# Norms by columns beside the last two output blocks of a stage, every second block of h by GpSimd and ScalarE

## The chip, the cores and the metric

The kernel runs on one core of a Trainium2 chip. The metric is the device time of one execution in microseconds (us); the times of several executions are given as median and span. "PE" is TensorE, "DVE" is VectorE, "ACT" is ScalarE, "POOL" is GpSimd, "SP" is the engine that issues most DMAs.

## The reference, cut to what matters

A backbone of two layers on 256 context tokens and 512 latent tokens, with a model width D of 1024. Cut to what the change touches:

```python
def rmsnorm(x, w):
    xf = x.astype(jnp.float32)
    y = xf * lax.rsqrt(jnp.mean(xf * xf, axis=-1, keepdims=True) + NORM_EPS)
    return (y * w.astype(jnp.float32)).astype(x.dtype)

for l in range(DEPTH):
    hx = modulate(rmsnorm(x, norm1_w[l]), mod_x[0], mod_x[1])      # h * (1 + scale) + shift
    hc = modulate(rmsnorm(ctx, norm1_w[l]), mod_c[0], mod_c[1])
    mix_x, mix_c = token_mixing(hx, hc, w_in[l], ...)
    x = x + mod_x[2] * (mix_x @ w_out[l])
    x = x + mod_x[5] * channel_mlp(modulate(rmsnorm(x, norm2_w[l]), mod_x[3], mod_x[4]), mlp_w1[l], mlp_w2[l])
    if not last:
        ctx = ctx + mod_c[2] * (mix_c @ w_out[l])
        ctx = ctx + mod_c[5] * channel_mlp(modulate(rmsnorm(ctx, norm2_w[l]), mod_c[3], mod_c[4]), mlp_w1[l], mlp_w2[l])
return rmsnorm(x, final_norm_w)
```

The context has a modulation of its own (`mod_c`). The last layer carries the latent tokens alone past its mixing. Everything is fp32; `channel_mlp` is a squared ReLU between two products.

## The kernel before

Tokens lie in columns: columns 0 to 255 are the context, 256 to 767 the latent tokens. The residual stream is eight tiles `X[k]` of 128 rows (features) and 768 columns (`NT`). Weights come in blocks of 128 output features.

**Products.** An fp32 product is made from fp32r parts. A weight block is split by ACT (`whi`, a rounded copy) and DVE (`wlo`, the rest) in halves of four 128-row blocks (`wsplit`, lines 463 to 475; `wload`, 478 to 489, also issues the block's DMA). The activations are split the same way into `hhi` and `hlo`. Each block k then takes three matmuls, hi times hi, lo times hi, hi times lo. A column segment is at most 512 wide, so 768 columns are two segments, 256 and 512 wide (`ALL`); in the last layer after its mixing there is one, of 512 (`LAT`). `gemm` (L492) runs over halves of the weights, segments, k and the three parts. `gemm_pair` (L506) makes two output blocks at once and has k as its outer loop, so that it can start on h of block 0 while block 1 is being made.

**Norms.** While the blocks n of a product are added to the residual stream (`residual`, L273), `sumsq` (L227) squares them on ACT and adds the squares on DVE; after block 7 two matmuls per segment with a matrix of ones (`nrm`) sum over the rows and spread the sum over all rows. `modulated` (L244) then makes `rstd` from it by a Ln and an Exp on ACT, and for each of eight blocks and each segment: `hy` (DVE, x times scale times rstd), `hhi` (ACT, hy plus shift, rounded), `hlo` (DVE, the rest). `hy` has two buffers (pool `tp`, tag `ta`), which the blocks take in turn. DVE makes two of the three steps.

**The four places.** A norm ends and an h begins at (a) the start of layer 0 (near 44 us of the span), where x is read from memory and the sums come from another path; (b) the second norm of layer 0 (606 us), between `w_out` and the MLP; (c) the first norm of layer 1 (1160 us), between the MLP and the input projection, whose first `gemm_pair` makes 32 gate columns and 128 columns of k; (d) the second norm of layer 1 (1590 us), with one segment. At (c) the tiles of layer 0's MLP give way to pools of layer 1.

**Other work there.** In layer 0 a generator `ada_sums` (L359) makes the modulation of layer 1 from 96 blocks of `ada_w` read by DMA: DVE instructions `adacc` over 128x1024, one or two to a block, are put between other work, a step at each `next(sums, None)`. At (a) ACT also issues the eight DMAs that save x to memory (`xd`, L625).

**Order.** Each engine runs its instructions in order. That order is set at build time by a list scheduler that takes the program's dependencies and pools; waits between engines are on semaphores that count finished instructions. So an instruction that waits holds up all that stands behind it on its engine.

Of the kernel before, what the change touches and what calls it, by code (L numbers as in the profile page):

```python
# [140 lines left out]
def flow_kernel(ctx, tc, t, out, dbg=None, stop=None):  # L141
# [85 lines left out]
    def sumsq(k, acc, segs, pl):  # L227

        cols = slice(segs[0][0], NT)
        sq = pl.tile([128, NT], F32, tag="sqa" if k == 0 else "tc", name="sq", bufs=1 if k == 0 else 2)  # L230
        act_(sq[:, cols], X[k][:, cols], AF.Square)
        if k in (0, 7):
            acc.append(sq)
        else:
# [4 lines left out]
        for i, sq in enumerate(acc):
            for c0, cn in segs:  # L240
                if i == 0:
                    o[bank(c0)] = ps("nrm")
                mm(o[bank(c0)][:, 0:cn], ones, sq[:, c0:c0 + cn], i == 0, i == 1)
        return o  # L244

    def modulated(l, which, segs, o, tp):
# [4 lines left out]
        V.tensor_scalar(out=sc, in0=mod[l][:, base + 8:base + 16, :], scalar1=1.0, scalar2=None, op0=ADD)
        tt(sc, sc, bc(prm[l][:, r0:r0 + 8], 2, 2), MUL)
        res = []
        r = tp.tile([128, GAP + 4], F32, tag="tb", name="rstd", bufs=2 - which)
        for c0, cn in segs:
            rr = r[:, c0:c0 + cn]
            act_(rr, o[bank(c0)][:, 0:cn], AF.Ln, scale=1.0 / D, bias=eps)
            act_(rr, rr, AF.Exp, scale=-0.5)
        for k in range(8):
            hi = hpool.tile([128, NT], F32R, tag="hi", name="hhi")  # L260
            lo = hpool.tile([128, NT], F32R, tag="lo", name="hlo")
            y = tp.tile([128, GAP + 4], F32, tag="ta", name="hy")
            for c0, cn in segs:
# [242 lines left out]
    def gemm_pair(w2, acts, segs, n):  # L506

        outs = [{bank(c0): ps("mm") for c0, cn in segs} for _ in n]
        for k in range(8):
            ahi, alo = acts[k]  # L510
            for i, w_ in enumerate(w2):
                whi, wlo = w_[k // 4]
                for c0, cn in segs:
                    for pi, (w, a) in enumerate(((whi, ahi), (whi, alo), (wlo, ahi))):
                        mm(outs[i][bank(c0)][0:n[i], 0:cn], w[:, k % 4, 0:n[i]], a[:, c0:c0 + cn],
                           start=(k == 0 and pi == 0), stop=(k == 7 and pi == 2))
        return outs

# [78 lines left out]
    for l in range(DEPTH):  # L597
# [23 lines left out]
        h = modulated(l, 0, ALL, nrm, tp)  # L621
        del nrm
# [9 lines left out]
        o, o_k0 = gemm_pair(ahead, h, ALL, (32, 128))  # L632
# [904 lines left out]
        acc = []  # L1537
# [1 line left out]
        for n in range(8):
# [2 lines left out]
            nrm = sumsq(n, acc, osegs, tp)
# [6 lines left out]
        h2 = modulated(l, 1, osegs, nrm, tp)  # L1549
        first = gemm_pair(w2, h2, osegs, (128, 128))  # L1550
        acc = []
        for fb in range(4):
            hid = []
            for f in range(8):
                if fb == 0 and f < 2:
                    o = first[f]
# [67 lines left out]
```

## Time and profile before

| what | value |
|---|---|
| median of 3 runs | 1973.41 us (1973.05 to 1975.29) |
| the profiled execution | 1960.3 us |
| its span (first to last instruction in the profile) | 1958.5 us |
| PE busy | 1881.4 us, 96% of the span |
| DVE busy | 1196.3 us, 61% |
| ACT busy | 754.2 us, 39% |
| POOL busy | 101.1 us, 5% |

The span is the part of an execution that the profile's rows cover. A busy share of PE says only that a matmul was under way; matmuls overlap, and a matmul at a lower clock counts as busy for longer. So what PE loses at one place is read from the distance between starts of its matmuls there.

### The profile page before, as it was taken

Reading aid. Unit: us, or ns where it says so; the run is one execution under the profiler, and the core shown is the slowest. Engines: PE = TensorE matmul, PEld = TensorE weight load, DVE = VectorE, ACT = ScalarE, POOL = GpSimd, SP = SyncE. Lnnn points to the kernel's source line nnn. Section 1 sums busy time; section 2 is a strip of 40 time slices with the busy share of each in tenths; the row PEclk is TensorE's granted clock in tenths of the full one; section 3 lists DMA queues with packets and bytes.
Section 4 is the critical chain, followed back from the end, with each engine's and each line's share of the span. In section 5 each row is a group of like instructions: output and inputs, shape, how many; then the busy total and the mean of one; then the engine's idle time right before and its main releaser. Section 6 shows DMA issues by size and latency. Waiting matters only on the chain.

```text
span 1958.5 us, 33935 instructions
## 1 busy us (share of the span) xinstructions
PE 1881.4 (96%) x14107; PEld 1539.8 (79%) x14107; DVE 1196.3 (61%) x2210; ACT 754.2 (39%) x1528; POOL 101.1 (5%) x163
## 2 busy tenths in 40 slices
PE   6999999999899999999999999999999999999998
PEld 3877778778777888888888878677777778888887
DVE  3878875666659566435535349788777754444443
ACT  4652234455424312312213236534355543333242
POOL 0021210000000000000000000212100000000001
PEclk8999989999799999999999999999999999999999
DMA  9220001111364345335423222201011323333332
GB/s 324 80 52 24 23 13 44 57 55 44 120 203 128 109 140 147 94 116 151 129 84 122 81 62 54 63 23 34 23 44 33 102 76 103 97 97 97 97 97 76
DMA packets 225634, 172.28 MB, mean 88 GB/s; under 512 B 19042, under 2 KB 207816, under 8 KB 225480
## 3 DMA queue, kind: packets, MB, share of 16 engines
q1 hardware_dynamic: 219104, 153.38, 26.5%
q10 hardware_dynamic: 4680, 10.70, 1.5%
q0 software_dynamic: 1696, 6.03, 0.9%
q8 instruction: 110, 1.80, 0.4%
q14 instruction: 44, 0.36, 0.1%
HBM read 162.75 MB, written 7.34 MB: 87 GB/s over the span
## 4 chain that ended last, share of the span: by engine, by line
PE 82%; DVE 10%; ACT 4%; DMA 3%; issue 1%; POOL 0%; DVEq 0%; ACTq 0%; SPq 0%; POOLq 0%
PE mm L179 63%; PE mmt L179 2%; PE num L179 1%; PE ops L179 1%; DVE kq L188 1%; DMA wst<-w_in 1%; PE pv L179 1%; DVE wlo L185 1%; PE yt L179 1%; DVE Y L185 1%; PE adaps L179 1%; PE pT L1340 1%; PE t L179 1%; PE Eps L179 1%; PE yps L179 1%
## 5 line engine op out<-in xcount | busy, mean ns | idle before, releaser
L182 ACT ACTIVATE whi<-wst 128x512 fp32r<-128x512 f32 (+1 forms) x388 | 241.7, 627 | 682.2 <-PE mm L179 623.5
L179 PE MATMUL mm<-hhi,whi 128*128 128x512 f32 (+3 forms) x1344 | 477.8, 361 | 12.8 <-ACT hhi L182 11.4
L179 PE MATMUL mm<-hlo,whi 128*128 128x512 f32 (+3 forms) x1344 | 479.4, 357 | 1.5 <-DVE hlo L188 1.3
L179 PE MATMUL mm<-hhi,wlo 128*128 128x512 f32 (+3 forms) x1344 | 475.3, 356 | 0.1
L185 DVE TENSOR_TENSOR wlo<-wst,whi 128x512 fp32r<-128x512 f32 (+1 forms) x388 | 265.1, 687 | 313.3 <-ACT whi L182 309.4
L179 PEld LDWEIGHTS mm<-hhi,whi 128*128 128x128 f32 (+1 forms) x1344 | 251.9, 188 | 55.4 <-ACT hhi L182 14.9
L179 PEld LDWEIGHTS mm<-hlo,whi 128*128 128x128 f32 (+1 forms) x1344 | 253.1, 188 | 39.9 <-DVE hlo L188 3.6
L179 PEld LDWEIGHTS mm<-hhi,wlo 128*128 128x128 f32 (+1 forms) x1344 | 252.2, 188 | 39.0 <-issue 2.8
L179 PE MATMUL mm<-fhi,whi 128*128 128x512 f32 (+1 forms) x784 | 276.0, 352 | 0.0
L179 PE MATMUL mm<-flo,whi 128*128 128x512 f32 (+1 forms) x784 | 276.0, 352 | 0.0
L179 PE MATMUL mm<-fhi,wlo 128*128 128x512 f32 (+1 forms) x784 | 274.6, 350 | 0.0
L188 DVE SCALAR_TENSOR_TENSOR x<-mm,mod,x 128x256 f32<-128x256 f32 (+1 forms) x122 | 79.7, 653 | 142.4 <-PE mm L179 142.3
L179 PEld LDWEIGHTS mm<-fhi,whi 128*128 128x128 f32 x784 | 148.4, 189 | 21.7 <-ACT whi L182 0.8
L179 PEld LDWEIGHTS mm<-fhi,wlo 128*128 128x128 f32 x784 | 148.1, 189 | 19.7
L179 PEld LDWEIGHTS mm<-flo,whi 128*128 128x128 f32 x784 | 148.4, 189 | 19.2
L188 DVE SCALAR_TENSOR_TENSOR adacc<-adw,scT,adacc 128x1024 f32<-128x1024 f32 x84 | 105.8, 1281 | 28.3 <-DMA adw<-ada_w 28.2
L185 DVE TENSOR_TENSOR flo<-r,fhi 128x768 fp32r<-128x768 f32 (+1 forms) x64 | 52.6, 824 | 39.2 <-ACT fhi L182 39.1
L182 ACT ACTIVATE fhi<-r 128x768 fp32r<-128x768 f32 (+1 forms) x64 | 47.2, 740 | 66.8 <-DVE r L185 66.8
L179 PE MATMUL mm<-mlo,whi 128*128 128x512 f32 (+1 forms) x192 | 71.0, 370 | 1.3 <-DVE mlo L185 1.3
L179 PE MATMUL mm<-mhi,whi 128*128 128x512 f32 (+1 forms) x192 | 70.6, 368 | 0.4 <-ACT mhi L182 0.4
L179 PE MATMUL mm<-mhi,wlo 128*128 128x512 f32 (+1 forms) x192 | 70.0, 365 | 0.0
L182 ACT ACTIVATE r<-mm 128x256 f32<-128x256 f32 (+1 forms) x96 | 49.1, 514 | 31.5 <-PE mm L179 31.5
(404 smaller groups left out, 2712.3 us busy)
## 6 DMA issues: line engine op xcount, KB each, us to landing
wst<-mlp_w SPq DMA_DIRECT2D x128, 512.0 KB, 4.0
adw<-ada_w SPq DMA_DIRECT2D x96, 512.0 KB, 4.3
wst<-w_in SPq DMA_DIRECT2D x44, 512.0 KB, 3.7
wst<-w_out SPq DMA_DIRECT2D x64, 128.0 KB, 3.1
xd<-x ACTq DMA_DIRECT2D x8, 384.0 KB, 3.5
x<-xd POOLq DMA_DIRECT2D x8, 384.0 KB, 5.2
xs<-x ACTq DMA_DIRECT2D x4, 512.0 KB, 6.9
wst<-w_in SPq DMA_DIRECT2D x8, 256.0 KB, 3.4
```

What stands on the lines that cost most here:

```text
L179: T.matmul(o, lhsT=l, rhs=r, start=start, stop=stop)
L182: S.activation(out=o, in_=i, func=f, **kw)
L185: (eng or V).tensor_tensor(out=o, in0=a, in1=b, op=op)
L188: V.scalar_tensor_tensor(out=o, in0=a, scalar=s, in1=b, op0=op0, op1=op1)
L1340: T.transpose(o[:, 256 * i + 128 * g:256 * i + 128 * g + 128], Ps[g][:, 128 * (i0 + i):128 * (i0 + i) + 128], ident)
```

## The change

- `sumsq` works per column segment and keeps one sum for each; the matmuls with ones move to `norm_sum`, called per segment. `modulated` is now called per segment, too.
- `last_pair` (new) makes the last two output blocks (6 and 7) of `w_out` in both layers, and of the second MLP product of layer 0, by columns: the first segment of both blocks, then the second segment of both. The norm of the first segment is issued with the second segment's products, its h behind them.
- Segments are now 512 latent columns, then 256 of the context (`LATF`), and at (d) two times 256 (`HALVES`). `gemm_pair` runs per segment, once for each, and h of the second segment is made beside the first segment's products.
- Every second block of h (odd k) is made in another way: GpSimd multiplies x by rstd, ACT scales and shifts it in place, ACT copies it rounded (`hhi`), DVE subtracts (`hlo`). Even blocks stay as they were. Of an odd block DVE now has one instruction, ACT two, GpSimd one.
- The steps of `ada_sums` left over are drained ahead of the last pair of layer 0's MLP; in the loop over `w_out` the eight steps are spread over six blocks rather than eight.

```diff
+LATF = ((256, 512), (0, 256))
-    def modulated(l, which, segs, o, tp):
+    def modulation(l, which):
...
-        r = tp.tile([128, GAP + 4], F32, tag="tb", name="rstd", bufs=2 - which)
...
-            y = tp.tile([128, GAP + 4], F32, tag="ta", name="hy")
-            for c0, cn in segs:
-                m = 1 if c0 == 0 else 0
-                s_ = slice(c0, c0 + cn)
...
+        def modulated(seg, o, pl, bufs):
...
+            act_(r, o[:, 0:cn], AF.Ln, scale=1.0 / D, bias=eps)
+            act_(r, r, AF.Exp, scale=-0.5)
+            for k in range(8):
...
+                y = pl.tile([128, GAP + 4], F32, tag="ta", name="hy", bufs=2)[:, 0:cn]
                 sh = mod[l][:, base + k, m:m + 1]
-                stt(y[:, s_], X[k][:, s_], sc[:, k, m:m + 1], r[:, s_], MUL, MUL)
-                act_(hi[:, s_], y[:, s_], AF.Identity, bias=sh)
-                stt(lo[:, s_], y[:, s_], sh, hi[:, s_].bitcast(F32), ADD, SUB)
+                if k % 2:
+                    tt(y, X[k][:, s_], r, MUL, eng=G)
+                    act_(y, y, AF.Identity, scale=sc[:, k, m:m + 1], bias=sh)
+                    act_(hi[:, s_], y, AF.Copy)
+                    tt(lo[:, s_], y, hi[:, s_].bitcast(F32), SUB)
+                else:
+                    stt(y, X[k][:, s_], sc[:, k, m:m + 1], r, MUL, MUL)
+                    act_(hi[:, s_], y, AF.Identity, bias=sh)
+                    stt(lo[:, s_], y, sh, hi[:, s_].bitcast(F32), ADD, SUB)
...
+    def last_pair(w2, acts, l, g, segs, acc, pl, mk):
...
+        for i, seg in enumerate(segs):
+            for n in (6, 7):
+                o = gemm(None, acts, (seg,), w2=w2[n - 6])
+                if i and n == 6:
+                    o_n = norm_sum(acc, segs[0])
+                if i and n == 7:
+                    h_ = mk(segs[0], o_n, pl, 1)
+                residual(o, l, n, g, (seg,))
+                sumsq(n, acc, ((i, seg),), pl)
+        return h_
...
-        h = modulated(l, 0, ALL, nrm, tp)
-        del nrm
+        if l == 0:
+            mk = modulation(0, 0)
+            h = mk(LATF[0], nrm[1], tp, 2)
+        first = gemm_pair(ahead, h, LATF[0], (32, 128))
+        mk(LATF[1], nrm[0], tp, 2)
+        first = [{1: a, 0: b} for a, b in zip(first, gemm_pair(ahead, h, LATF[1], (32, 128)))]
...
+        steps = HALVES if last else LATF
-        for n in range(8):
+        for n in range(6):
...
-            for _ in range((2, 1, 1, 1, 1, 1, 1, 0)[n]):
+            for _ in range((2, 1, 1, 1, 1, 2)[n]):
                 next(sums, None)
...
+        mk = modulation(l, 1)
+        h2 = last_pair([wload([t["w_out"][l][:, 128 * n:128 * n + 128]], MIXK) for n in (6, 7)], mh, l, 16, steps, acc, tp, mk)
...
-        first = gemm_pair(w2, h2, osegs, (128, 128))
+        first = [gemm_pair(w2, h2, steps[0], (128, 128))]
+        mk(steps[1], norm_sum(acc, steps[1]), tp, 1)
+        first.append(gemm_pair(w2, h2, steps[1], (128, 128)))
...
+            w2 = [wload([t["mlp_w2"][l][3072:4096, 128 * n:128 * n + 128]]) for n in (6, 7)]
+            if not last:
+                for _ in sums:
+                    pass
+                mk = modulation(l + 1, 0)
+                h = last_pair(w2, hid, l, 40, LATF, acc, tp, mk)
+                nrm = {0: norm_sum(acc, LATF[1])}
```

VectorE at (b), before (names are tile and buffer number; `hy` and `hlo` of two blocks in turn, L188 is the helper for scalar-tensor-tensor, x2 two such instructions in a row, `adacc` the sums of `ada_sums`):

```order
L188 SCALAR_TENSOR_TENSOR x_6486<-mm_7077,mod0_121,x_6486 128x512
L185 TENSOR_TENSOR wlo_7368<-wst_7361,whi_7367 128x512
L188 SCALAR_TENSOR_TENSOR adacc_7344<-adw_7501,scT_89,adacc_7344 128x1024 x2
L188 SCALAR_TENSOR_TENSOR hy_7166<-x_6479,sc_7156,rstd_7159 128x256
L188 SCALAR_TENSOR_TENSOR hy_7175<-x_6480,sc_7156,rstd_7159 128x256
L188 SCALAR_TENSOR_TENSOR hy_7166<-x_6479,sc_7156,rstd_7159 128x512
L188 SCALAR_TENSOR_TENSOR hlo_7165<-hy_7166,mod0_121,hhi_7164 128x256
L188 SCALAR_TENSOR_TENSOR hlo_7174<-hy_7175,mod0_121,hhi_7173 128x256
L188 SCALAR_TENSOR_TENSOR hy_7175<-x_6480,sc_7156,rstd_7159 128x512
L188 SCALAR_TENSOR_TENSOR hlo_7165<-hy_7166,mod0_121,hhi_7164 128x512
L188 SCALAR_TENSOR_TENSOR adacc_7344<-adw_7573,scT_89,adacc_7344 128x1024
```

and with the change, from the same place on (L189 is now that helper, L186 the one for tensor-tensor):

```order
L186 TENSOR_TENSOR wlo_7420<-wst_7417,whi_7419 128x512
L189 SCALAR_TENSOR_TENSOR x_6503<-mm_7147,mod0_121,x_6503 128x256
L189 SCALAR_TENSOR_TENSOR adacc_7400<-adw_7557,scT_89,adacc_7400 128x1024
L189 SCALAR_TENSOR_TENSOR hlo_7176<-hy_7177,mod0_121,hhi_7175 128x512
L186 TENSOR_TENSOR hlo_7182<-hy_7183,hhi_7181 128x512
L189 SCALAR_TENSOR_TENSOR hy_7190<-x_6498,sc_7029,rstd_7172 128x512
L186 TENSOR_TENSOR wlo_7424<-wst_7417,whi_7423 128x512
L189 SCALAR_TENSOR_TENSOR adacc_7400<-adw_7629,scT_89,adacc_7400 128x1024
L189 SCALAR_TENSOR_TENSOR hlo_7189<-hy_7190,mod0_121,hhi_7188 128x512
L186 TENSOR_TENSOR hlo_7195<-hy_7196,hhi_7194 128x512
L189 SCALAR_TENSOR_TENSOR hy_7203<-x_6500,sc_7029,rstd_7172 128x512
L189 SCALAR_TENSOR_TENSOR adacc_7400<-adw_7629,scT_89,adacc_7400 128x1024
```

Before, one `adacc` stands between the instructions of the first h blocks; now three or four stand among those of the first four blocks, and the `hlo` of an odd block (a L186 row that reads `hy` and `hhi` alone) stands behind one or two of them.

ScalarE at (b) with the change (L183 is the helper for activations; an `hy` made from `hy` is the in-place scaling of an odd block, an `hhi` with one name its rounded copy):

```order
L183 ACTIVATE rstd_7172<-nrm_7140,cst_85 128x512
L183 ACTIVATE rstd_7172<-rstd_7172 128x512
L183 ACTIVATE whi_7419<-wst_7417 128x512
L183 ACTIVATE hy_7183<-hy_7183,mod0_121,sc_7029 128x512
L183 ACTIVATE hhi_7175<-hy_7177,mod0_121 128x512
L183 ACTIVATE hhi_7181<-hy_7183 128x512
L183 ACTIVATE sq_7228<-x_6503 128x256
L183 ACTIVATE whi_7423<-wst_7417 128x512
L183 ACTIVATE hy_7196<-hy_7196,mod0_121,sc_7029 128x512
L183 ACTIVATE hhi_7188<-hy_7190,mod0_121 128x512
```

Before, ACT had one `hhi` per block and segment there; now three instructions stand for two blocks, in the order odd scaling, even `hhi`, odd `hhi`.

TensorE at (c) with the change (`mm_11876` is the gate product, 32 columns of weights, `mm_11877` the k product of the same segment, 128 columns; `mm_11965` and `mm_11966` are those of the second segment):

```order
L180 MATMUL mm_11876<-hhi_11815,wlo_11863 32x512
L180 MATMUL mm_11876<-hhi_11822,whi_11862 32x512
L180 MATMUL mm_11876<-hlo_11823,whi_11862 32x512
L180 MATMUL mm_11876<-hhi_11822,wlo_11863 32x512
L180 MATMUL mm_11876<-hhi_11828,whi_11862 32x512
L180 MATMUL mm_11876<-hlo_11829,whi_11862 32x512
L180 MATMUL mm_11876<-hhi_11828,wlo_11863 32x512
L180 MATMUL mm_11877<-hhi_11783,whi_11868 128x512
L180 MATMUL mm_11877<-hlo_11784,whi_11868 128x512
L180 MATMUL mm_11965<-hhi_11783,whi_11858 32x256
L180 MATMUL mm_11965<-hlo_11784,whi_11858 32x256
```

Before, the two products of a block followed each other for each k; now the gate product runs over all eight blocks of the first segment ahead of the first matmul of the k product.

## Rows read from the trace of the kernel before

**Rows 1.** The page: the span, and busy time, share and instructions of each engine.
```profile
span 1958.5 us, 33935 instructions
PE 1881.4 (96%) x14107; PEld 1539.8 (79%) x14107; DVE 1196.3 (61%) x2210; ACT 754.2 (39%) x1528; POOL 101.1 (5%) x163
```

**Rows 2.** Windows: length, then busy us (instructions) of PE, PEld, DVE, ACT, POOL, PE clock, DMA, GB/s.
```profile
44.00:52.00 8.00, 7.40 (x26) 5.11 (x27) 8.00 (x16) 3.90 (x8) 0.20 (x2) 0.56 0.95 315
612.00:622.00 10.00, 9.17 (x48) 7.26 (x48) 10.00 (x19) 5.29 (x10) 0.00 (x0) 1.00 0.13 47
```

**Rows 3.** PE timeline, the norm's first matmuls at (b), (c), (d): start, us, instruction.
```profile
606.20 1.03 PE L179 MATMUL nrm<-sq,ones 128*128 128x256 f32 x3
...
1160.39 1.03 PE L179 MATMUL nrm<-sq,ones 128*128 128x256 f32 x3
...
1590.39 1.02 PE L179 MATMUL nrm<-sq,ones 128*128 128x512 f32 x2
```

**Rows 4.** PE timeline, first product of h at (a) to (d), [idle before, releaser].
```profile
44.41 0.42 PE L179 MATMUL mm<-hhi,whi 128*32 128x256 f32 x1 [4.21 <-ACT hhi L182]
...
611.67 0.38 PE L179 MATMUL mm<-hhi,whi 128*128 128x256 f32 x1 [1.84 <-ACT hhi L182]
...
1166.10 0.31 PE L179 MATMUL mm<-hhi,whi 128*32 128x256 f32 x1 [2.21 <-ACT hhi L182]
...
1596.22 0.96 PE L179 MATMUL mm<-hhi,whi 128*128 128x512 f32 x3 [2.98 <-ACT hhi L182]
```

**Rows 5.** PE timeline, the last matmuls of gemm_pair or of the third product.
```profile
64.21 0.40 PE L179 MATMUL mm<-hhi,wlo 128*128 128x512 f32 x1
...
638.72 0.39 PE L179 MATMUL mm<-hhi,wlo 128*128 128x512 f32 x1
638.95 0.28 PE L179 MATMUL mm<-hhi,whi 128*128 128x256 f32 x1
639.06 0.28 PE L179 MATMUL mm<-hlo,whi 128*128 128x256 f32 x1
...
1185.13 0.40 PE L179 MATMUL mm<-hhi,wlo 128*128 128x512 f32 x1
...
1614.14 0.39 PE L179 MATMUL mm<-hhi,wlo 128*128 128x512 f32 x1
```

**Rows 6.** ACT timeline around the four places.
```profile
48.98 0.81 ACTq L625 DMA_DIRECT2D xd<-x  x2
...
1165.56 0.50 ACT L182 ACTIVATE hhi<-hy,mod 128x256 fp32r<-128x256 f32 x1
...
1593.28 0.69 ACT L182 ACTIVATE rstd<-nrm,cst 128x512 f32<-128x512 f32 x1 [1.22 <-PE nrm L179]
1594.00 0.63 ACT L182 ACTIVATE rstd<-rstd 128x512 f32<-128x512 f32 x1
...
1598.31 1.38 ACT L182 ACTIVATE hhi<-hy,mod 128x512 fp32r<-128x512 f32 x2 [1.48 <-DVE hy L188]
...
1604.39 0.61 ACT L182 ACTIVATE whi<-wst 128x512 fp32r<-128x512 f32 x1
```

**Rows 7.** DVE timeline at (b) and (d).
```profile
611.92 0.87 DVE L188 SCALAR_TENSOR_TENSOR hlo<-hy,mod,hhi 128x256 fp32r<-128x256 f32 x2
...
614.03 1.28 DVE L188 SCALAR_TENSOR_TENSOR adacc<-adw,scT,adacc 128x1024 f32<-128x1024 f32 x1
...
1599.07 1.41 DVE L188 SCALAR_TENSOR_TENSOR hlo<-hy,mod,hhi 128x512 fp32r<-128x512 f32 x2
```

**Rows 8.** POOL groups by line and form: count, busy us, mean ns, idle before.
```profile
L185 POOL TENSOR_TENSOR N<-E,cst 128x512 f32<-128x512 f32 x12 | 15.5, 1293 | 46.2 <-ACT E L182 46.1
```

**Rows 9.** Timeline, POOL and DVE in the mixing of layer 0; DVE alone at (d).
```profile
164.15 2.73 POOL L185 TENSOR_TENSOR Nl<-N,Nh 64x512 f16<-64x512 f32 x2 [16.95 <-PE nw L179]
164.61 1.25 DVE L185 TENSOR_TENSOR wlo<-wst,whi 128x512 fp32r<-128x512 f32 x1
...
1603.90 0.69 DVE L185 TENSOR_TENSOR wlo<-wst,whi 128x512 fp32r<-128x512 f32 x1 [1.21 <-PE mm L179]
```

More of the change, by code (lines that the diff above doesn't have):

```diff
@@ L504, in gemm, with gemm_pair @@
         return outs
-    def gemm_pair(w2, acts, segs, n):
-        outs = [{bank(c0): ps("mm") for c0, cn in segs} for _ in n]
+    def gemm_pair(w2, acts, seg, n):
+        outs = [ps("mm") for _ in n]
+        c0, cn = seg
         for k in range(8):
             ahi, alo = acts[k]
-            for i, w_ in enumerate(w2):
+            for o, n_, w_ in zip(outs, n, w2):
                 whi, wlo = w_[k // 4]
[L513 to L516, printed above, removed]
-        return outs
+                for pi, (w, a) in enumerate(((whi, ahi), (whi, alo), (wlo, ahi))):
+                    mm(o[0:n_, 0:cn], w[:, k % 4, 0:n_], a[:, c0:c0 + cn],
+                       start=(k == 0 and pi == 0), stop=(k == 7 and pi == 2))
+        return outs
+    def last_pair(w2, acts, l, g, segs, acc, pl, mk):
[9 more added lines that the diff above has]
+        return h_
     def gemm_tok(l, c0, pairs, hk, evac):
@@ L631, in flow_kernel @@
         zg = temp("ta")
-        o, o_k0 = gemm_pair(ahead, h, ALL, (32, 128))
+        o, o_k0 = first
         evac(zg[0:32], o, ALL, 32)
@@ L1536, in flow_kernel @@
             nc.gpsimd.dma_start(out=X[k][:, ow], in_=xd[k, :, ow])
[L1537 removed]
+        acc = {}
         sums = ada_sums(todo, adp)
[L1539 removed]
+        steps = HALVES if last else LATF
+        for n in range(6):
             o = gemm([t["w_out"][l][:, 128 * n:128 * n + 128]], mh, osegs, order=MIXK, w2=w_next.pop() if w_next else None)
             residual(o, l, n, 16, osegs)
[L1542 to L1543 removed]
+            sumsq(n, acc, tuple(enumerate(steps)), tp)
+            for _ in range((2, 1, 1, 1, 1, 2)[n]):
                 next(sums, None)
@@ L1555, in flow_kernel @@
                 if fb == 0 and f < 2:
-                    o = first[f]
+                    o = [(x[f], seg) for x, seg in zip(first, steps)]
                 else:
                     o = gemm([t["mlp_w1"][l][:, 1024 * fb + 128 * f:1024 * fb + 128 * f + 128]], h2, osegs)
+                    o = [(o[bank(c0)], (c0, cn)) for c0, cn in osegs]
                 r = tp.tile([128, NT], F32, tag="tc", name="r")
-                for c0, cn in osegs:
-                    act_(r[:, c0:c0 + cn], o[bank(c0)][:, 0:cn], AF.Relu)
+                for x, (c0, cn) in o:
+                    act_(r[:, c0:c0 + cn], x[:, 0:cn], AF.Relu)
                 tt(r[:, ow], r[:, ow], r[:, ow], MUL)
@@ L1568, in flow_kernel @@
                 next(sums, None)
-            tail = last and fb == 3
-            for n in range(6 if tail else 8):
+            for n in range(6 if fb == 3 else 8):
                 o = gemm([t["mlp_w2"][l][1024 * fb:1024 * fb + 1024, 128 * n:128 * n + 128]], hid, osegs)
                 residual(o, l, n, 40, osegs)
-                if tail:
+                if fb == 3 and last:
                     finish(n, acc, tp, *LAT[0])
                 elif fb == 3:
-                    nrm = sumsq(n, acc, osegs, tp)
+                    sumsq(n, acc, tuple(enumerate(LATF)), tp)
                 next(sums, None)
-            if tail:
-                w2 = [wload([t["mlp_w2"][l][3072:4096, 128 * n:128 * n + 128]]) for n in (6, 7)]
+            if fb < 3:
+                continue
+            w2 = [wload([t["mlp_w2"][l][3072:4096, 128 * n:128 * n + 128]]) for n in (6, 7)]
[5 more added lines that the diff above has]
+                nrm = {0: norm_sum(acc, LATF[1])}
+            else:
                 for seg in HALVES:
```

54 lines of the change are left out of this document (28 added, 26 removed).

## The prediction

> **What bounds the kernel now.** I read the page first: PE is busy 96% of a span of 1958.5 us, DVE 61%, POOL 5% [rows 1]. So only time in which PE waits, or steps slower than it can, is to be had. The page cannot say where that is; the PE timeline can. Full steps between matmul starts are 0.23 us for 512 columns and 0.115 us for 256 [rows 5]. The change touches four places, and I compare each with what its matmuls need at those steps: 8.3 us for 24 matmuls of both widths (one output block over 768 columns).
>
> At (a) gemm_pair's 48 matmuls of each width need 16.6 us and take from 44.41 to 64.44: 3.4 us more, behind a first wait of 4.2 [rows 4, 5]; the granted clock is 0.56 there and DVE is busy for 8.00 us of 8 [rows 2]. At (b) the norm starts at 606.20 and the third product ends at 638.95: 32.75 us for 2.6 of norm matmuls (about 0.22 and 0.43 for each half of one, two halves a matmul [rows 3]) and 24.9 of products, 5.2 lost. At (c), 1160.39 to 1185.36, 25.0 us for 2.6 and 16.6: 5.8 lost. At (d), 1590.39 to 1614.37, 24.0 us for 1.7 and 16.4: 5.9 lost. The first product's wait ends on ACT's `hhi` in all four, 1.84 to 4.21 us [rows 4]; after it h comes slowly. At (b) DVE is busy all of the 10 us after the norm [rows 2]: DVE makes h there. In all, some 24 us are lost, 1.2% of the span: the most that the change can gain, and less by (a)'s first wait, which it does not touch.
>
> **The column split.** It takes matmuls of 5.7 us (24 of 256 columns for each of n = 6 and 7) out from before the norm and puts them beside it. Call T0 the moment when the first segment of n = 7 is through: 5.7 us before the norm's start of today, so 600.5 at (b), 1154.7 at (c), 1584.7 at (d) [rows 3]. From T0 the kernel before takes 38.4, 30.7 and 29.7 us to the ends named above. The norm of the first segment waits for n = 6's second half on PE, 2.8 us, then takes 1.7 itself (0.9 for 256 columns), then Ln 0.69 and Exp 0.63 on ACT [rows 6] (0.9 together for 256 columns): `rstd` at T0+6.1, at (d) T0+4.9. Only 2.8 us of products are then left to cover h. The split's other additions cost little: the same columns are multiplied, but at (d) as 256 wide (0.115 for half of 0.23), under 0.5 us in all.
>
> **How fast h comes now.** An odd block is a chain through three engines, and `hy` still has two buffers, of which the odd blocks always get the second. So GpSimd cannot start block 3 before DVE has finished block 1's `hlo`. Nothing of two odd blocks overlaps, and the chain is the period for two blocks. For 512 columns: GpSimd's product 1.29, the nearest row being its `N` of the same shape [rows 8]; ACT's scaling and the even `hhi` that stands behind it, 1.38 as two `hhi` take [rows 6]; the rounded copy, 0.54 more, as a `whi` of 0.61 less its overlap [rows 6]; `hlo` 0.69, as `wlo` [rows 9]; three handovers of 0.05. That is 4.05.
>
> To this I add a collision. When DVE's `wlo` ran beside GpSimd's `Nl`, it took 1.25 instead of 0.69 [rows 9]: two-input work of the two engines does not run side by side. An even `hy` on DVE (0.66 a step, half of a pair of 1.41 [rows 7]) is released by the same event as GpSimd's product. I let one wait for the other: 4.7 us a pair. The row bounds it: nothing, to the whole 0.66. I take the whole, since `wlo` was held for nearly its own length. [...]
>
> For 256 columns the same chain is 0.40 + 0.63 (half of 1.29) + 0.50 + 0.40 + 0.30 + 0.40 + 0.15 = 2.8 [rows 6, 7, 8]. PE needs 12 matmuls for two blocks, 2.7 us at 512 and 1.4 at 256. So h is the limit throughout, by 2.0 and 1.4 us a pair. Before, DVE made h at 2.8 us for two blocks of 512 columns, four steps of 0.7 [rows 7].
>
> **Place by place.**
> (a) No split here, the first wait stays. On ACT five `xd` issues stand between the first `hhi` and the first odd scaling, 0.4 us each, 2.0 in all [rows 6]. With `hy` from 43.0, as now, block 1 is whole at 49.0 (0.66 + 1.29 + 2.0 + 0.72 + 0.61 + 0.69). ACT's even `hhi` is not in the chain here, so three pairs of 4.0 and four of 2.5 follow, and 0.5 of matmuls: 71.5 against 64.4, **+7.1**.
> (b) The scheduler put up to two `adacc` of 1.2 us [rows 7] into each pair on DVE. The first pair takes 4.7, two of them (2.4) and a `whi` (0.5): T0+13.7. Three more pairs with 0.8 us each that the chain does not hide, 5.5: T0+30.2. Four pairs of the second segment at 3.0: T0+42.2. Behind the last `hlo` stand 1.4 of the pair and 4.1 of the third product: T0+47.7 against 38.4, **+9.3**.
> (c) Block 1 at T0+10.8, three pairs of 4.7: T0+24.9. The second block of weights waits for the last `hlo` of this segment, since its pool lies where the old stage's `hy` was; so up to then PE has only the 32-wide gate products (24 steps of 0.23, 5.5 us). Then `whi`, 0.8 with handovers, 24 steps of 512 and 48 of 256 columns, 11.2, and 1.8 for steps at half clock after so idle a stretch (as (d) now: 18.15 us from its first product for 16.4 [rows 4, 5]): T0+38.7 against 30.7, **+8.0**.
> (d) Block 1 at T0+7.9, three pairs and four of 2.9: T0+28.2, and 4.1 behind: T0+32.3 against 29.7, **+2.6**.
>
> The sum is 7.1 + 9.3 + 8.0 + 2.6 = **+27.0**. The profiled execution took 1960.3, 13.1 below the median of the runs, 1973.4; it would go to 1987.3. I put the difference on the median: 1973.4 + 27.0, **2000 us**. Differences within 0.2%, 3.9 us, count as none.
>
> **Rivals.**
> *No collision.* GpSimd's product starts at once and costs 1.29: 0.66 less for each of twelve pairs of 512 columns and 0.4 for each of sixteen of 256, 14.3 less: 1986. For it: the collision rows are of other shapes and another stage. Against: both engines wait for the same release here.
> *The cover works, a faster kernel.* GpSimd and ACT take half of h from DVE, and a pair comes in under the 2.7 us that PE needs; then only the first pair is late, by 4.7 less 2.7. (b), (c) and (d) lose 2.0 us each in place of 5.2, 5.8 and 5.9, (a) stays: 10.9 less, 1963. It decides at a period of 2.7 us; the chain is 4.05 before any collision, and only a third `hy` buffer or shorter instructions could bring it there. For it: DVE was the limit at (b) and has two instructions fewer for two blocks.
> *Between the two.* With the even `hhi` out of the chain's way a period would be about 3.4, half way between 4.05 and 2.7, and so half way between 1986 and 1963: about 1975, no change.
> *The clock stays low.* [...] If it falls in all four places while h comes in steps, the dense matmuls behind the last `hlo`, 5.5 + 9 + 4 us, run partly at twice the step: some 8 us more, 2008.
>
> **Chances.** Forecast 0.45, no collision 0.25, clock low 0.10, cover works 0.11, between 0.09. Slower is the sum of the first three, 0.80; within 0.2% 0.09; faster 0.11. The range leaves out the faster case and half of what is between, and reaches at the top past the low clock: 1974 to 2014.
>
> **What would show it.** Right: in the changed kernel's PE timeline pairs of blocks come 4 to 5.5 us apart at 512 columns, with waits on `hhi` or `hlo` of odd blocks; POOL's `hy` starts right after an odd `hlo`; at (c) the first 128-wide product stands 24 us behind T0. Wrong: pairs at 2.7 us, PE without gaps, POOL's products overlapping the odd block before. If GpSimd's product takes much less than 1.29, or DVE's instructions keep their length beside it, the sizes fall first.

## The result and the profile after

The changed kernel takes 2000.94 us, median of 4 runs (1992.20 to 2005.93); the kernel before, beside it, 1973.23 (1972.71 to 1975.29). The ratio is 1.0134, 95% interval 1.0097 to 1.0170: slower by 1.3%. The forecast was 2000. The profiled execution took 1992.2 us, its span is 31.9 us longer than that of [rows 1].

The page of the changed kernel, span and engines (PE, PEld, DVE, ACT, POOL):

```profile
span 1990.4 us, 34272 instructions
...
PE 1889.3 (95%) x14207; PEld 1543.8 (78%) x14207; DVE 1204.2 (61%) x2214; ACT 774.8 (39%) x1596; POOL 140.3 (7%) x195
```

The work went to POOL and ACT as intended: POOL has 39 us more, ACT 21. DVE is not relieved: 8 us more, although 32 products of h are POOL's now. What DVE kept takes longer; how much is counted below, at `odd_on_dve`.

Where the time went is read from PE's first matmul of each stage. Stages in us, each from the start of one such matmul to that of the next; "fc" is the forecast for the place.

| stage | before | after | difference | fc |
|---|---|---|---|---|
| (a) to the gates' transposes, layer 0 | 64.5 | 75.5 | +11.0 | +7.1 |
| mixing of layer 0 | 459.8 | 458.8 | -1.0 | |
| (b) `w_out` to the second MLP product | 157.5 | 166.6 | +9.1 | +9.3 |
| rest of the MLP and (c), to the gates of layer 1 | 503.6 | 511.0 | +7.3 | +8.0 |
| mixing of layer 1 | 358.9 | 361.7 | +2.8 | |
| (d) `w_out` to the second MLP product | 97.2 | 98.8 | +1.6 | +2.6 |
| the rest | 317.0 | 318.1 | +1.1 | |

Place (c) shows the mechanism most plainly. PE timeline of the changed kernel (start, us, instruction, idle before it and what ended it), the first product of every second block of h, and the first 128-wide one:

```profile
1182.67 0.41 PE L180 MATMUL mm<-hhi,whi 128*32 128x512 f32 x1 [0.97 <-ACT hhi L183]
...
1187.32 0.41 PE L180 MATMUL mm<-hhi,whi 128*32 128x512 f32 x1 [2.09 <-ACT hhi L183]
...
1191.95 0.42 PE L180 MATMUL mm<-hhi,whi 128*32 128x512 f32 x1 [2.50 <-ACT hhi L183]
...
1196.59 0.64 PE L180 MATMUL mm<-hhi,whi 128*32 128x512 f32 x1 [2.24 <-ACT hhi L183]
...
1199.51 0.63 PE L180 MATMUL mm<-hhi,whi 128*128 128x512 f32 x1
```

Two blocks come every 4.64 us, where the forecast had 4.7, and PE waits over 2 us for each pair. The wait before, 2.21 us, stood there once [rows 4]. The 128-wide product starts only after the last block, and at half clock: granted 0.50 from 1198.66 to 1200.37, with 0.43 us to a step around it where 0.23 is a full one [rows 5].

One round of that chain, on POOL, DVE and ACT of the same kernel:

```profile
1179.87 1.29 POOL L186 TENSOR_TENSOR hy<-x,rstd 128x512 f32<-128x512 f32 x1 [530.50 <-ACT rstd L183]
...
1184.09 1.72 POOL L186 TENSOR_TENSOR hy<-x,rstd 128x512 f32<-128x512 f32 x1 [2.62 <-DVE hlo L186]
```

```profile
1179.82 1.89 DVE L189 SCALAR_TENSOR_TENSOR hy<-x,sc,rstd 128x512 f32<-128x512 f32 x1 [1.65 <-ACT rstd L183]
...
1183.32 0.68 DVE L186 TENSOR_TENSOR hlo<-hy,hhi 128x512 fp32r<-128x512 f32 x1
1183.92 0.74 DVE L189 SCALAR_TENSOR_TENSOR hy<-x,sc,rstd 128x512 f32<-128x512 f32 x1
...
1187.97 0.68 DVE L186 TENSOR_TENSOR hlo<-hy,hhi 128x512 fp32r<-128x512 f32 x1
```

```profile
1185.84 0.81 ACT L183 ACTIVATE hy<-hy,mod,sc 128x512 f32<-128x512 f32 x1 [1.02 <-POOL hy L186]
1186.56 0.71 ACT L183 ACTIVATE hhi<-hy,mod 128x512 fp32r<-128x512 f32 x1
1187.17 0.61 ACT L183 ACTIVATE hhi<-hy 128x512 fp32r<-128x512 f32 x1
```

POOL's second product is released by DVE's `hlo` of the odd block before (the bracket names it) and starts at 1184.09, while DVE's even `hy` runs from 1183.92 to 1184.66. It takes 1.72 us, 0.43 over the 1.29 of the first. In the first pair both are released by `rstd`. By the rows DVE's `hy` starts 0.05 us ahead of POOL's product, and yet DVE pays: `hy` takes 1.89 us in place of 0.74, while the product keeps its 1.29. Then ACT scales, makes the even `hhi` and the odd `hhi`, and DVE's `hlo` at 1187.97 releases POOL's next product, which starts 4.64 us after the one before.

So in each pair one of the two waits for the other. The product that came 0.17 us after `hy` was held up by it, for 0.43 us of the 0.57 that `hy` had left, and the `hy` beside the first product ended only 0.55 us after that one. The order of the starts in the rows does not settle which one waits: with starts 0.05 us apart the one that the rows put later went first.

### The profile page after: what moved, and what is told of

Its sections match the earlier page's. It is cut to its first block, busy times and chain, and to the rows that moved or that the text cites. A ratio compares the mean times of both kernels' runs of the same rounds, so it can differ in the third digit from the quotient of the medians.

```text
span 1990.4 us, 34272 instructions
## 1 busy us (share of the span) xinstructions
PE 1889.3 (95%) x14207; PEld 1543.8 (78%) x14207; DVE 1204.2 (61%) x2214; ACT 774.8 (39%) x1596; POOL 140.3 (7%) x195
## 3 DMA queue, kind: packets, MB, share of 16 engines
q1 hardware_dynamic: 219104, 153.38, 25.9%
## 4 chain that ended last, share of the span: by engine, by line
PE 77%; DVE 9%; issue 5%; ACT 4%; DMA 2%; POOL 2%; ACTq 0%; DVEq 0%; POOLq 0%
PE mm L180 59%; PE mmt L180 2%; PE num L180 1%; POOL hy L186 1%; PE ops L180 1%; PE pv L180 1%; PE yt L180 1%; DVE Y L186 1%; PE Eps L180 1%; PE t L180 1%; PE pT L1372 1%; DVE wlo L186 1%; PE yps L180 1%; DMA xs<-x 1%; PE rps L180 1%
## 5 line engine op out<-in xcount | busy, mean ns | idle before, releaser
L180 PE MATMUL mm<-hhi,whi 128*128 128x512 f32 (+3 forms) x1360 | 485.3, 359 | 30.1 <-ACT hhi L183 28.7
L183 ACT ACTIVATE whi<-wst 128x512 fp32r<-128x512 f32 (+1 forms) x388 | 241.0, 627 | 663.2 <-PE mm L180 609.8
L180 PE MATMUL mm<-hlo,whi 128*128 128x512 f32 (+3 forms) x1360 | 484.9, 357 | 4.7 <-DVE hlo L189 3.5
L186 DVE TENSOR_TENSOR wlo<-wst,whi 128x512 fp32r<-128x512 f32 (+1 forms) x388 | 266.4, 691 | 319.6 <-ACT whi L183 316.8
L189 DVE SCALAR_TENSOR_TENSOR x<-mm,mod,x 128x256 f32<-128x256 f32 (+1 forms) x124 | 80.2, 646 | 139.0 <-PE mm L180 138.8
L189 DVE SCALAR_TENSOR_TENSOR adacc<-adw,scT,adacc 128x1024 f32<-128x1024 f32 x84 | 110.5, 1335 | 29.4 <-DMA adw<-ada_w 29.4
L186 POOL TENSOR_TENSOR hy<-x,rstd 128x256 f32<-128x256 f32 (+1 forms) x32 | 39.4, 1231 | 706.4 <-ACT rstd L183 646.0
L186 DVE TENSOR_TENSOR flo<-r,fhi 128x768 fp32r<-128x768 f32 (+1 forms) x64 | 52.6, 825 | 40.0 <-ACT fhi L183 40.0
L183 ACT ACTIVATE fhi<-r 128x768 fp32r<-128x768 f32 (+1 forms) x64 | 47.3, 740 | 69.2 <-DVE r L186 69.1
```

The source lines that it names most:

```text
L180: T.matmul(o, lhsT=l, rhs=r, start=start, stop=stop)
L183: S.activation(out=o, in_=i, func=f, **kw)
L186: (eng or V).tensor_tensor(out=o, in0=a, in1=b, op=op)
L189: V.scalar_tensor_tensor(out=o, in0=a, scalar=s, in1=b, op0=op0, op1=op1)
```

## The experiments

The first four take the change apart. "Before" in each is a run of the kernel before on the same chip. Differences of a place are against the first profile of the kernel before. How far a place moves by itself is seen in the profiles that leave it as it was: five have 64.3 to 66.7 us for (a) and 156.3 to 160.8 for (b), four have 503.6 to 504.7 for the rest of the MLP and (c), two 97.2 and 97.3 for (d).

**Split alone: all blocks of h on VectorE** (`split_only`).

```diff
-                if k % 2:
+                if False:
                     tt(y, X[k][:, s_], r, MUL, eng=G)
```

> The change with every block of h made as before (two instructions on VectorE, one on ScalarE); the column split, the drained sums and the order stay. Theory of the forecast (the chain over GpSimd is what costs): h comes again at 2.8 us for two blocks of 512 columns and about 1.6 for 256; the start of layer 0 is as before to within 2 us, the other three places gain a little (0 to 3 us each, the first waits shrink): 1966 to 1974 us, ratio 0.996 to 1.000. Rival (the split itself costs: the sums packed into the h phase, the weights that wait at the start of layer 1): 1983 us or more, ratio over 1.005.

1967.69 us against 1971.13, ratio 0.9982 (0.9962 to 1.0002). As the theory has it; the rival falls. By stages of its profile: (a) +1.4, (b) +0.7, MLP and (c) +0.9, (d) -4.2; the first three are no more than such a place moves by itself.

**GpSimd alone: the kernel before with odd blocks by GpSimd and ScalarE** (`gp_only`).

```diff
-                stt(y[:, s_], X[k][:, s_], sc[:, k, m:m + 1], r[:, s_], MUL, MUL)
...
+                if k % 2:
+                    tt(y[:, s_], X[k][:, s_], r[:, s_], MUL, eng=G)
+                    act_(y[:, s_], y[:, s_], AF.Identity, scale=sc[:, k, m:m + 1], bias=sh)
+                    act_(hi[:, s_], y[:, s_], AF.Copy)
+                    tt(lo[:, s_], y[:, s_], hi[:, s_].bitcast(F32), SUB)
```

> The kernel before with odd blocks of h by GpSimd and ScalarE, and nothing else of the change. Theory of the forecast: a pair of blocks over 768 columns takes 5.3 to 5.6 us in place of 4.2 to 4.5, at (d) 4.7 for 512 in place of 2.8: some 4 to 5 us more at each of the four places, 1985 to 1993 us, ratio 1.006 to 1.010. Rival (the split costs, not the way h is made): within 0.2% of before. A third view (GpSimd relieves VectorE): faster by 5 us or more.

1988.52 us, ratio 1.0071 (1.0047 to 1.0094), in the theory's range. The places: (a) +5.1, (b) +6.0, MLP and (c) +3.3, (d) +4.3. At (d), where 512 columns stand alone, POOL's products start 4.66 us apart, the same period with no split in the kernel:

```profile
1625.28 1.72 POOL L185 TENSOR_TENSOR hy<-x,rstd 128x512 f32<-128x512 f32 x1 [2.93 <-DVE hlo L185]
1629.94 1.73 POOL L185 TENSOR_TENSOR hy<-x,rstd 128x512 f32<-128x512 f32 x1 [2.93 <-DVE hlo L185]
1634.61 1.73 POOL L185 TENSOR_TENSOR hy<-x,rstd 128x512 f32<-128x512 f32 x1 [2.94 <-DVE hlo L185]
```

So the whole loss comes with the way over GpSimd, and it costs more with the split (1.0134 against 0.9982) than without (1.0071). A likely reason, by full steps of 0.23 and 0.115 us and not tested by itself: with both segments at once PE has 4.1 us of matmuls to a pair at (a), (b) and (c), with the 512 columns alone 2.8.

**A third buffer for hy** (`hy3`): tag and tile by `k % 3`, all else as in the change.

```diff
-                y = pl.tile([128, GAP + 4], F32, tag="ta", name="hy", bufs=2)[:, 0:cn]
+                if k % 3 < 2:
+                    y = pl.tile([128, GAP + 4], F32, tag="ta", name="hy", bufs=2)[:, 0:cn]
+                elif bufs == 2:
+                    y = pl.tile([128, GAP + 4], F32, tag="tc", name="hy", bufs=1)[:, 0:cn]
+                else:
+                    y = pl.tile([128, 512], F32, tag="hyx", name="hy", bufs=1)[:, 0:cn]
```

> The change with a third buffer for hy (blocks take three in turn), so that GpSimd's product of an odd block can start before the odd block ahead of it is done. Theory of the forecast: the pair period falls from 4.7 us to what the engines need with the collision, about 3.2 for 512 columns and 2.0 for 256; 1978 to 1988 us, ratio 1.002 to 1.008. Rival (the collision of GpSimd and VectorE alone sets the pace, whatever the buffers): pairs stay at 4 us or more, 1994 us or more, ratio over 1.010.

1985.65 us, ratio 1.0063 (1.0031 to 1.0096): within the theory's range, the rival's is left. POOL is now released by the `hlo` of an even block (L189), and its products at (c) come 2.3 to 3.6 us apart in place of 4.64, though each but the first still takes longer than 1.29. At (a) they stay 4.0 to 4.7 apart, for a reason that `gp_fixed` shows below. At (c):

```profile
1186.65 1.67 POOL L186 TENSOR_TENSOR hy<-x,rstd 128x512 f32<-128x512 f32 x1 [2.04 <-DVE hlo L189]
1188.95 1.72 POOL L186 TENSOR_TENSOR hy<-x,rstd 128x512 f32<-128x512 f32 x1 [0.63 <-DVE hlo L189]
```

**The odd block's first product on VectorE** (`odd_on_dve`).

```diff
-                    tt(y, X[k][:, s_], r, MUL, eng=G)
+                    tt(y, X[k][:, s_], r, MUL)
```

> The change with the first product of an odd block on VectorE in place of GpSimd (0.6 us in place of 1.29, and no collision); ScalarE's two passes, the two buffers and all else stay. Theory of the forecast: a pair at 512 columns comes at about 3.3 us (0.6 + 0.72 + 0.66 + 0.54 + 0.69 and handovers), at 256 about 2.1: 1976 to 1984 us, ratio 1.001 to 1.005. Rival (the second pass on ScalarE and the two buffers cost most, not GpSimd): 1990 us or more, ratio over 1.008.

1978.22 us, ratio 1.0032 (1.0015 to 1.0050), as the theory has it. With ScalarE's second pass and the two buffers kept, GpSimd's length and the collision together are about three quarters of the loss (1.0134 to 1.0032). What is left lies between this and the split alone (0.9982): an odd block's longer way over ScalarE. By the stages half of that is at (a), +7.2 here and +1.4 with the split alone, where the saves of x stand on ScalarE too.

This run also counts what the move did to VectorE. Summed over the trace, the 32 first products took 16.7 us on VectorE here. In the change they are gone from it, and its other instructions take 17.0 us longer in sum: the even `hy` 6.9, the `adacc` 4.5, the rest in smaller parts. All that was moved away came back.

The next two measure one term of the sum each.

**rstd in PSUM for VectorE** (`psum_rstd`).

```diff
-            act_(r, o[:, 0:cn], AF.Ln, scale=1.0 / D, bias=eps)
-            act_(r, r, AF.Exp, scale=-0.5)
+            rp = o[:, 0:cn]
+            act_(rp, rp, AF.Ln, scale=1.0 / D, bias=eps)
+            act_(r, rp, AF.Exp, scale=-0.5)
+            act_(rp, rp, AF.Exp, scale=-0.5)
...
-                    stt(y, X[k][:, s_], sc[:, k, m:m + 1], r, MUL, MUL)
+                    stt(y, rp, sc[:, k, m:m + 1], X[k][:, s_], MUL, MUL)
```

> The change with rstd kept in PSUM as well: ScalarE writes it twice, GpSimd reads the copy in SBUF, VectorE's hy of even blocks reads the one in PSUM, so that of its inputs only x is in SBUF. All else stays, the third instruction for rstd (0.6 us) comes on top. Theory of the forecast (GpSimd's product and the even hy hold each other up): GpSimd's product goes from 1.72 us back to 1.29 for 512 columns and from 0.92 to 0.63 for 256, hy stays at 0.74 beside it; pairs come 0.4 and 0.3 us closer, twelve and sixteen of them, 10 us in all: about 1990 us, ratio 1.007 to 1.010. At the second norm of layer 0 less, since the sums on VectorE still read SBUF twice. Rival (the longer times of GpSimd's product come from something else, ScalarE's in-place pass or memory traffic): the same 1.72, ratio 1.012 or more.

The mechanism shows, the size does not: 1993.27 us, ratio 1.0127 (1.0099 to 1.0155), above the theory's range and on the rival's side, and no gain over the change can be told. At (c) the second product of POOL and the even `hy` of DVE now run side by side, each at its own length (POOL, then DVE):

```profile
1182.96 1.29 POOL L186 TENSOR_TENSOR hy<-x,rstd 128x512 f32<-128x512 f32 x1 [2.57 <-DVE hlo L186]
```

```profile
1182.80 0.75 DVE L189 SCALAR_TENSOR_TENSOR hy<-nrm,sc,x 128x512 f32<-128x512 f32 x1
```

That is the collision of these two, shown, and the rival's reason falls: with one input of `hy` out of SBUF it is gone (1.29 and 0.75), and pairs come 4.2 us apart there. At (b), where POOL's products came 6.28, 5.25 and 5.35 us apart, they come 5.11, 4.38 and 4.92. At 256 columns the period at (d) goes from 2.88 to 2.71, POOL's product from 0.92 to 0.75 (the change, then this run):

```profile
1638.17 0.92 POOL L186 TENSOR_TENSOR hy<-x,rstd 128x256 f32<-128x256 f32 x1 [1.97 <-DVE hlo L186]
```

```profile
1639.19 0.75 POOL L186 TENSOR_TENSOR hy<-x,rstd 128x256 f32<-128x256 f32 x1 [1.97 <-DVE hlo L186]
```

But at (a) POOL's products stay at 1.75 us: the scheduler puts the even `hlo`, which reads two tiles of SBUF, behind the odd one there, and in the changed kernel the product that starts 0.16 us after such an `hlo` (51.34, 0.75 long) takes 1.73. At (b) `wlo` and `adacc` stay as they were; that they still hold POOL's product up is an estimate: of 17.6 us for all twelve products, less three of 1.75 and the four at (c) of about 1.29, 7.2 are left for five. Against the change's profile (b) is 5.2 us shorter, (c) 1.1, (d) 0.8; the mixing stages took 7.3 us more in this profile, of which more below.

**The saves of x from SyncE** (`xd_sp`), one profiled execution.

```diff
-            nc.scalar.dma_start(out=xd[k, :, ow], in_=X[k][:, ow])
+            nc.sync.dma_start(out=xd[k, :, ow], in_=X[k][:, ow])
```

> The change with the eight saves of x at the start of each layer issued by SyncE in place of ScalarE. Theory (five issues in a row on ScalarE stood between the first rounded block and the first odd scaling at the start of layer 0, 3.3 us): the start of layer 0 ends 2.5 to 3.5 us earlier, the gates' transposes near 72.5 us in place of 75.5. Rival (the first odd block waits for GpSimd and VectorE anyway): within 0.5 us of 75.5.

The gates' transposes start at 72.7 us in place of 75.5: 2.8 us, as the theory has it. The span is the change's all the same, 1990.2 us for 1990.4: the mixing of layer 0 took 2.2 us more. ACT at (a), in the changed kernel:

```profile
45.41 0.72 ACT L183 ACTIVATE hhi<-hy,mod 128x512 fp32r<-128x512 f32 x1 [0.89 <-DVE hy L189]
45.41 3.33 ACTq L657 DMA_DIRECT2D xd<-x  x5
48.79 0.81 ACT L183 ACTIVATE hy<-hy,mod,sc 128x512 f32<-128x512 f32 x1 [2.66 <-DMA xd<-x]
```

and in this run:

```profile
45.86 0.72 ACT L183 ACTIVATE hhi<-hy,mod 128x512 fp32r<-128x512 f32 x1 [1.98 <-DVE hy L189]
46.49 0.80 ACT L183 ACTIVATE hy<-hy,mod,sc 128x512 f32<-128x512 f32 x1
```

The last ones try for a faster version, and ask what else moved.

**All three costs taken down** (`gp_fixed`): the diffs of hy3, psum_rstd and xd_sp together.

> The change with all three costs of the GpSimd way taken down: a third buffer for hy, rstd in PSUM for VectorE, the saves of x issued by SyncE. Theory (these three are the cost, and they add up): the third buffer alone gave 1.0063; the saves take 2.8 us more off and PSUM some 2 to 5: 1978 us or less, ratio 1.002 to 1.004, still behind VectorE alone. Rival (with a third buffer the pairs are bound by ScalarE or by what is left of the collision, so the two others add nothing): 1.006 or more.

1978.93 us, ratio 1.0054 (1.0036 to 1.0072), between the two forecasts. In its stages (b) +1.3, MLP and (c) +2.1 and (d) -2.2 are near the split alone; (a) keeps +5.8. Its mixing of layer 1 is 9.3 us longer than in the first profile of before. So the costs named are most of the loss at (b) to (d). At (a) the rows point at the order on ScalarE:

```profile
45.83 0.80 ACT L183 ACTIVATE hy<-hy,mod,sc 128x512 f32<-128x512 f32 x1
49.08 0.81 ACT L183 ACTIVATE hy<-hy,mod,sc 128x512 f32<-128x512 f32 x1 [2.45 <-POOL hy L186]
49.80 0.61 ACT L183 ACTIVATE hhi<-hy 128x512 fp32r<-128x512 f32 x1
50.32 0.71 ACT L183 ACTIVATE hhi<-hy,mod 128x512 fp32r<-128x512 f32 x1
```

Block 1 is scaled by 46.63, but its rounded copy, at 49.80, stands behind the scaling of block 3, which waits for POOL. Block 1 is whole at 51.14, hardly earlier than in the change (51.42), although the saves of x are out of the way. The even `hhi` of block 2 (50.32) stands behind that scaling, too, and its `hlo` frees POOL's next buffer: so POOL's next products again come 4.0 to 4.1 us apart. No run with another order there was made, so what it costs is not shown.

**The split at (d) alone** (`d_split`) **and with GpSimd there** (`d_split_gp`): the kernel before, with `last_pair`, `modulation` and the per-segment `gemm_pair` of the change used in the last layer's second norm; the first with the condition `k % 2` set to `False` as above.

```diff
+        if last:
+            mk = modulation(l, 1)
+            h2 = last_pair([wload([t["w_out"][l][:, 128 * n:128 * n + 128]], MIXK) for n in (6, 7)], mh, l, 16, HALVES, acc, tp, mk)
...
+        if last:
+            first = [gemm_pair_seg(w2, h2, HALVES[0], (128, 128))]
+            mk(HALVES[1], norm_sum(acc, HALVES[1]), tp, 1)
+            first.append(gemm_pair_seg(w2, h2, HALVES[1], (128, 128)))
```

> The kernel before with the column split at the second norm of layer 1 alone, two halves of 256 columns, h made on VectorE as before; nothing else of the change. Theory: that is the one place where the split pays when VectorE makes h (no sums beside it, no weights that wait, 4 us gained there in the profile of the split alone): 1967 to 1970 us, ratio 0.997 to 0.999. Rival (what is gained there comes back as a lower clock or a later wait): 0.9995 or more.

> The kernel before with the change at the second norm of layer 1 alone, odd blocks by GpSimd and ScalarE. Theory of the forecast: this place by itself is 1.5 to 3 us slower than before, since pairs of 256 columns come 2.9 us apart: 1973 to 1977 us, ratio 1.000 to 1.002. Rival (the places act on each other, and this one by itself gains as with VectorE): ratio 0.9985 or less.

With VectorE 1968.97 us, ratio 0.9990 (0.9972 to 1.0009): at the border of what was expected, and not to be told from no change. The stage (d) is 2.6 us shorter in its profile. With GpSimd 1973.65, ratio 1.0026 (1.0004 to 1.0047), above the expected range, which the interval still meets: the stage is 3.2 us longer. The sign is as the theory has it. By the stages the two ways differ by 5.8 us at this one place, with the same split.

**The split at (c) and (d)** (`cd_split`): as d_split, and `last_pair` after layer 0's MLP with the per-segment start of layer 1.

> The kernel before with the column split at two places, the first and the second norm of layer 1, h made on VectorE as before. Theory: the profile of the split alone gained 4.2 us at the second norm and 0.8 at the first, and lost at the two places of layer 0, which stay as before here: 5 us less, 1964 to 1968 us, ratio 0.9965 to 0.9985. Rival (what these places gain is within what the clock takes in other stages): 0.999 or more.

1967.49 us, ratio 0.9991 (0.9974 to 1.0009): the rival's side. (d) gains 4.2 us in its profile. (c) with the MLP ahead of it is 0.9 longer, as it is in `d_split`, which leaves it untouched (1.0): nothing gained or lost there. No version that was run beats the kernel before clear of the noise; the split alone comes nearest.

**The kernel before once more** (`before_again`), one profiled execution, no edit.

> The kernel before, unchanged, once more with a profile. In the profiles so far the mixing of layer 0, whose TensorE order is nearly the same in all, lasts 459 to 470 us, that of layer 1 359 to 368, by short stretches at half clock at differing places. If these fall by chance in each execution, this profile differs from the first one of the same kernel by a us or more in one of the two stages; if they belong to the kernel, it repeats 459.8 and 358.9 to within 0.5 us.

Its span is 1963.7 us, the first one's 1958.5. The mixing of layer 1 takes 363.2 us where it took 358.9, though all 3776 PE instructions of that stage come in the same order: the first part of the expectation holds. Windows of the two profiles (length; PE, PEld, DVE, ACT, POOL busy; granted clock; DMA share; GB/s), first the kernel before as in [rows 1], then its second profile:

```profile
1400.00:1421.00 21.00, 19.48 (x271) 17.17 (x271) 12.92 (x36) 8.93 (x13) 3.65 (x6) 1.00 0.10 27
1421.00:1432.00 11.00, 10.89 (x91) 10.62 (x90) 8.50 (x17) 1.94 (x6) 0.00 (x0) 1.00 0.19 49
```

```profile
1400.00:1421.00 21.00, 19.48 (x269) 16.87 (x269) 12.88 (x36) 9.02 (x13) 3.66 (x6) 1.00 0.10 27
1421.00:1432.00 11.00, 11.00 (x53) 10.59 (x53) 9.30 (x18) 1.11 (x3) 0.00 (x0) 0.53 0.10 27
```

PE is as busy in both, but for 11 us the granted clock is 0.53 in place of 1.00, and 53 matmuls go through in place of 91. In both, PE had waited 1.52 us for DVE just ahead of it. So the same wait was followed by a clock of 1.00 in one execution and of 0.53 in the next, where the stage took 4.4 us more; no run here shows what decides it.

## Why the prediction was right

The sum of the four places was 27.0; they took 29.0 in the profile. The median of the runs moved by 27.7. The mechanism and the sizes of the places came out; that the median fell within 1 us of the forecast is luck. The two profiles differ by 31.9 us, the four runs of the change by 13.7, and errors of both signs at the places, and in the chain below, cancel in part.

- **The chain of two odd blocks, 4.05 us, plus the collision, 0.66.** Right: 4.64 us at (c), 4.66 at (d) without the split. The rival without a collision had 4.05; rstd in PSUM brings the period to 4.2, so what the collision costs the chain is 0.43, and the chain itself is some 0.15 longer than forecast. At 256 columns it is the same: 0.40 was put in for the collision and 2.4 for the other steps, and 0.17 and 2.7 were measured; POOL's product by itself took 0.75 there, where half of 1.29 had been put in. The two errors nearly cancel. With the measured sizes the rival's price, 14.3 us for twelve and sixteen pairs, would be some 8 (an estimate). `psum_rstd` does not test that price: it left the collision at (a) and, by the estimate above, part of it at (b). At the three other places its profile is 7.1 us shorter than the change's; its time (1.0127) could not be told from the change's.
- **(b), 5.5 us a pair with the sums between.** Measured 5.3 for the second and third pair. How the sums come in is a collision too. POOL's and DVE's rows of the second pair:

```profile
623.85 2.32 POOL L186 TENSOR_TENSOR hy<-x,rstd 128x512 f32<-128x512 f32 x1 [4.08 <-DVE hlo L186]
```

```profile
624.96 2.30 DVE L189 SCALAR_TENSOR_TENSOR adacc<-adw,scT,adacc 128x1024 f32<-128x1024 f32 x1
```

  POOL's product, 1.29 alone, waits for `hy` (623.70, 0.74 long) and then for `wlo` (624.36, 0.68), and `adacc`, 1.28 us alone [rows 7], waits for POOL. I had charged it to DVE's own queue: right size, in part another reason.
- **(c), the second weights.** Right: the first 128-wide product stands behind all eight blocks, at half clock (granted 0.50), +7.3 for +8.0. The `whi` that it waits for starts at 1197.95 on ACT, just behind DVE's last `hlo` of the segment (1197.24 and 0.68 long); that the place of the pool is the reason was not tested apart. The product stands 25.9 us behind T0 (1173.65 in the changed kernel); the sum for (c) has 25.7, and the 24 among its signs does not follow from it.
- **(d).** +1.6 for +2.6. Pairs are 2.9 us apart, as forecast. That the first wait and the third product cost 1.0 less wasn't traced further.
- **(a).** +11.0 for +7.1: the step that failed is "five `xd` issues stand between the first `hhi` and the first odd scaling, 0.4 us each, 2.0 in all". They took 3.33 us and the scaling followed at 48.79 only, 3.4 us after the `hhi`; without them there (a) is 2.8 us shorter. A sixth put the rounded copy off by another 0.46. A further part, not measured by itself: POOL's first product began at 43.28 and held DVE's second `sc`, 0.17 us alone, for 1.27, so that the even `hy` began at 44.62 in place of 43.0. In all block 1 was whole at 51.42 where the sum has 49.0, 2.4 us of the 3.9. The periods behind it were as forecast, 4.0 to 4.3 and 2.1 to 2.9, 0.7 more in sum; the last 0.9 us passed between the last `hlo` and the transposes. TensorE did not wait for blocks all this time: behind block 1 it ran from 50.74 to 63.16 without a wait over 0.3 us, at a granted clock of 0.50 from 44 to 52 us and 0.69 from 52 to 60, where the kernel before has 0.56 and 1.00. At 63.16 it waited again, 0.85 us, so the blocks set the end.
- **Not foreseen:** +1.1 us in the rest, in all seven runs that use GpSimd for h and in none of the others. At the first block of the final norm (DVE and POOL of the changed kernel):

```profile
1946.34 1.61 DVE L595 TENSOR_SCALAR x<-x,prm 128x512 f32<-128x512 f32 x1 [0.16 <-ACT sq L183]
1946.39 1.28 POOL L186 TENSOR_TENSOR sqa<-sqa,sq 128x512 f32<-128x512 f32 x1 [307.30 <-ACT sq L183]
```

  In the kernel before:

```profile
1915.54 0.48 DVE L567 TENSOR_SCALAR x<-x,prm 128x512 f32<-128x512 f32 x1 [0.16 <-ACT sq L182]
```

```profile
1915.64 1.53 POOL L185 TENSOR_TENSOR sqa<-sqa,sq 128x512 f32<-128x512 f32 x1 [365.24 <-ACT sq L182]
```

  There POOL paid; here the turn went the other way, and PE waits for DVE's. The rows put DVE's start 0.10 us ahead of POOL's there and 0.05 here. Why the order turned isn't shown.
- **The two mixing stages**, +1.8 together, are within what two profiles of one kernel differ by (1.6 and 4.4 us).

The rival on the other side, that the cover works, fell with its own condition: it needed a period under 2.7 us. In the change it was 4.64; even with three buffers POOL's products came 2.3 to 3.6 us apart at (c), 3.0 in the mean. The rival with a low clock in all four places fell too: the granted clock was 0.59 from 44 to 60 us at (a), but 0.96 from 600.5 to 648.2 at (b), 0.91 from 1173.65 to 1212 at (c) and 1.00 from 1590 to 1660 at (d). For the doubled step that it counts with, the trace has 0.43 us in place of 0.23 where 0.50 was granted.

## What to carry to other kernels

Before work is moved from a busy engine to an idle one, follow one item through all engines that it then passes, with the number of buffers: with two buffers taken in turn by two kinds of blocks, each kind has one, and the sum of the chain is its period (4.64 us here), however idle each engine is. Look at the order on the engines in between, too: a step that is ready stands behind one that waits, as block 1's rounded copy did in `gp_fixed`, ready at 46.63 and run at 49.80. And count the partner's loss: in this kernel VectorE and GpSimd, both reading SBUF, took turns, and the 16.7 us "moved to GpSimd" came back whole, as 17.0 us in longer instructions on VectorE. Where two profiles of one kernel differ by 0.3% (1958.5 and 1963.7 us here), judge an edit by the stages that it touches, against how far those move by themselves, and only then by the total.

## What was not expected of the hardware

- A small instruction on VectorE waited as long as a large one: `sc`, 128x16 with 0.17 us alone, took 1.27 beside POOL's product (1.27), 1.10 more, where the `hy` of 0.74 took 1.15 more beside one of 1.29; and an instruction with a single tensor input (`x<-x,prm`, 0.48 alone) took 1.61 beside POOL's `sqa` of 1.28. In this kernel the collision isn't confined to two-input instructions.
- The clock: in stages that no edit touched, the mixing of layer 0 took between 458.8 and 470.2 us in thirteen profiles, that of layer 1 between 358.9 and 368.1. The two ends of layer 0 are the change and `hy3`, whose 4429 PE instructions there keep nearly the same order; the granted clock over the stage is 0.96 in the one and 0.94 in the other. Where two profiles of one kernel were laid side by side, the difference was a stretch at half clock, 0.53 for 1.00 over 11 us, behind a wait of 1.52 us that both had.
